# A decoder layer on one core: weight loads, running sums and sample loads around the scan's first group

## The chip, the cores and the metric

The kernel runs on one core of one Trainium2 chip. The metric is the time of one execution on the device in microseconds (us). A core has TensorE (matrix products, PE in the profile; PEld are its weight loads), VectorE (DVE), ScalarE (ACT), GpSimd (POOL) and SyncE (SP), which here only issues DMAs. Each engine works through its own instructions in order and waits on semaphores for the others.

## The reference

One inference step of one layer of a hybrid decoder for two groups of tokens at once: a prompt of 512 tokens and 8 samples of one token each, d_model 1024, all in float32. What matters here is branch B, a state space scan over 32 heads in 8 groups:

```python
proj = h @ w_in                                   # u | z | xBC | dt | gates
xbc  = silu(causal_conv(xbc))                     # 4 taps, x | B | C
dt   = softplus(dt_raw + dt_bias); dA = dt * A    # A = -exp(A_log)
# prompt: chunks of 128 tokens, per group
Acs   = cumsum(dA)                                # "running sums"
decay = exp(Acs[l] - Acs[s]) for s <= l
y_diag = ((C B^T) * decay) @ (x * dt)
states = B^T (exp(Acs[end] - Acs) * x * dt)
h      = h * exp(Acs[end]) + states               # from chunk to chunk
y_off  = C h_prev * exp(Acs)
# samples: one recurrent step from a given state (8 x 32 x 64 x 128)
y = (y_diag + y_off + D * x); y = rmsnorm(y * silu(z)) @ w_ssd_proj
```

A pooling mixer (branch A), the gated sum of the branches, an output projection and a SwiGLU feed-forward network follow, with adaLN modulation throughout. Outputs are both groups' results and the new pooling, convolution and scan states.

## The kernel before, in words

Activations lie transposed: channels on the 128 partitions, the 512 + 8 tokens in a row of 520. Every large product is made of columns: 128 output channels times the 1024 input channels (8 blocks) times 520 tokens in two halves. Float32 is kept by splitting both sides in two rounded parts and adding three products. So each weight block of 128 x 1024, a *unit* of 512 KB, goes the same way: a DMA into a buffer `raw` (L107; there are three, `NRAW`), a cast to the upper part on ScalarE (`whi`, L116), a subtraction on VectorE for the lower part (`wlo`, L117), which frees the buffer, and 48 matrix products on TensorE (L129).

All work stands in a list `plan` of steps with the units that each needs. `perform` goes through it and calls `ahead(n, m)` before each step: the first `n` units are loaded and split, and of the next `m` only the loads are issued. `n` is two units beyond those that the step needs; `m` is `W["loads"]`, which `sp_order(True)` sets to 2 in the middle of group 0.

The order on TensorE is written out everywhere. From `start` to the end of the scan, ScalarE, VectorE and GpSimd are kept to the written order too (`ordered`). SyncE is kept to it from `sp_order(True)` to `sp_order(False)` (`fetched`); before that a planner orders its DMAs by its own estimates.

`start` normalises and modulates the input and works through the first three columns (dt and the two x columns of group 0) block by block. It calls `ahead(3)` before the last three blocks, so the units 0 to 2 (B and C of group 0, the first x column of group 1) are split there. The memory of `start` is then reused: `cvs`, the samples' convolution states (L599), is loaded there, and GpSimd makes `cpre` of it (L608).

After that a loop over the eight groups g of the scan lists these steps: the columns x0, x1 (`xg`), B (`bt`), C (`ct`), each followed by a convolution (`conv`: ScalarE empties the result into `xb` and `v`, L642 and L643, VectorE adds three taps, L647, and the tail, `end`, runs with the next column), and two gate columns zz of the group before. Between the columns stand the steps of three generators:

- `scan(g)` (`step`): transposes (L723, L733), `xdt` (L728) and `xde` (L730), C B^T masked (L740, L742), chunk states (L762 to L769), scores times decays (L748, for group 0 all four together in `scores_first`), products into y (L787, L789, L793).
- `decays(g)` (`decay`): per chunk the exponentials of the running sums on ScalarE (L682 to L694). They need `dec`, the group's running sums broadcast to all partitions, which `dec_load(g)` (L674) loads from DRAM, 1 MB. Odd groups use the tile `aa`, even ones the tile `dec`.
- `sample(g)` (`part`), six steps: write the samples' B and C rows to DRAM (`dbc`, L815 to L818); load half of the states and the C rows (`h`, L803, and `cc`, L804); multiply on GpSimd (L808); reduce on VectorE (L812) and load the other half; multiply; reduce.

The running sums themselves come from `dt_parts`: a chain on VectorE, a write to DRAM (`dacs`, L575), and four DMAs of very small pieces, `dtx` (L585). `tokens_dt` turns them for the scan (`tok`, L618 and L620). `begin(0)` then loads the running sums of groups 0 and 1 one behind the other. Buffers that limit the order: three `raw`, two PSUM tiles `m` for the columns, four PSUM banks `b` for everything else.

Of the kernel before, what the change touches and what calls it, by code (L numbers as in the profile page):

```python
# [52 lines left out]
def tile_decoder(ctx: ExitStack, tc: tile.TileContext, I: dict, O: dict):  # L53
    nc = tc.nc
    ctx.enter_context(tc.manual_schedule(engines={mybir.EngineType.PE}))
    LOOK = 2
# [30 lines left out]
    def urgent():  # L87
        return tc.high_priority(offset=URGENT)
# [75 lines left out]
    def todo(fn, *units):  # L164
        plan.append((units, fn))

    W = {"made": [], "raws": {}}

    def ahead(n, m=0):

        queue, made, raws = W["queue"], W["made"], W["raws"]
        for i in range(len(made), min(n, len(queue))):
            u = queue[i]
            src, pool = (*u, None)[:2] if isinstance(u, tuple) else (u, None)
            with urgent() if count[0] > NU else nullcontext():
                raw = raws.pop(i) if i in raws else load(src)
                made.append(parts(raw, pool))
        for i in range(len(made), min(n + m, len(queue))):
            u = queue[i]
            if i not in raws:  # L180
                raws[i] = load(u[0] if isinstance(u, tuple) else u)

    def perform():
        queue = W["queue"] = [u for us, _ in plan for u in us]
        made = W["made"]
        at = 0
        for us, fn in plan:
            ahead(at + len(us) + (LOOK if at else 0), W.get("loads", 0))
            got = [made[at + i] for i in range(len(us))]
            for i in range(len(us)):  # L190
                made[at + i] = None
            at += len(us)
            fn(*got)
        plan.clear()
# [237 lines left out]
    raws = [ada_rows(0)]  # L432
    wraw = [load(w) for w in (win(72), X0(0), X1(0))]

    def start():
        sp = st
        RB = sp.tile([P, T], F32, name="RB")
        acc = sp.tile([P, T], F32, name="acc1")
        for s in range(1, len(SLICES)):
            raws.append(ada_rows(s))  # L440
        for k in range(KD):
            add_square(sp, acc, xT[:, k], 0, T, k == 0)
        nc.vector.tensor_scalar(cwh, pv[:, PV["cw"][0] : PV["cb"][1]], 0.5, None, ALU.mult)
        ends = {}

        def ada(s, ks=range(KD)):
            m0, m1 = SLICES[s]
            n, q = P, m1 - m0
            if ks[0] == 0:
                ends[s] = bank()  # L450
            for k in ks:
                ada_mm(ends[s], raws[s][:, k], k, n, k == 0, k == KD - 1, 2 * q)
            if ks[-1] == KD - 1:
                with urgent():
                    ends[s] = ada_end(ends[s], n, lambda i: (U_SC1, U_SH1)[i // q] + m0 + i % q, sp, 2 * q)

        def normed(k):
            xn = sp.tile([P, T], F32, tag="xn", name=f"xn{k}", bufs=3)
            (nc.vector if k % 2 == 0 else nc.gpsimd).tensor_tensor(xn, xT[:, k], RB, ALU.mult)
            return xn  # L460

        def modded(s):
            m0, m1 = SLICES[s]
            with urgent():
                ends[s]()
                a1 = mod[:, U_SC1 + m0 : U_SC1 + m1]
                nw = V["n1w"][:, m0:m1].unsqueeze(2).broadcast_to([P, m1 - m0, 9])
                nc.vector.scalar_tensor_tensor(a1, a1, 1.0, nw, ALU.add, ALU.mult)

        def rows(*ks):  # L470
            hs = []
            for k in ks:
                h = sp.tile([P, T], F32, tag="h", name=f"h{k}", bufs=2)
                modulate(h, xn.pop(k), mod[:, U_SC1 + k], mod[:, U_SH1 + k])
                nc.scalar.copy(hh[:, k], h)
                hs.append(h)
            for k in ks:
                if k + 2 < KD:
                    xn[k + 2] = normed(k + 2)
            for k, h in zip(ks, hs):  # L480
                nc.vector.tensor_tensor(hl[:, k], h, hh[:, k].bitcast(F32), ALU.subtract)  # L481

        def products(k, tiles=range(3)):
            for o, w in [(outs[i], ws[i]) for i in tiles]:
                product(o, w, k, hh[:, k], hl[:, k], k == 0, k == KD - 1)


        def warm(n):
            b = bank()
            for _ in range(n):  # L490
                nc.tensor.matmul(b[:, 0:256], cold[:, 0:P], cold, start=True, stop=True)

        warm(WARM[0])
        r = rstd_start(acc, 1024, range(5))
        w0 = parts(wraw[0], "st")
        ada(0)
        modded(0)
        rstd_end(r, range(5), RB)
        warm(WARM[1])
        xn = {k: normed(k) for k in range(2)}  # L500
        rows(0)
        ws = [w0] + [parts(w, "st") for w in wraw[1:]]
        outs = [both(main()), both(main()), pair()]
        products(0, [0])
        ada(1, range(4))
        products(0, [1, 2])
        ada(1, range(4, KD))

        def rest(s):
            modded(s)  # L510
            rows(*range(*SLICES[s]))

        rest(1)
        ada(2)
        products(1)
        rest(2)
        products(2)
        ada(3)
        products(3)
        modded(3)  # L520
        ada(4)
        rows(5, 6)
        products(4)
        rest(4)
        ahead(3)
        for k in range(5, KD):
            products(k)
        first["ps"] = outs
        closed(st_)
# [136 lines left out]
    def dec_load(g):  # L666

        if g >= NG:
            return
        if g % 2:  # L670
            dec = G["aa"][:, 4:8].rearrange("p a b -> p (a b)")[:, 0:2048].rearrange("p (c h l) -> p c h l", c=4, h=4)
        else:
            dec = S["sp"].tile([P, 4, 4, P], F32, tag="dec", name=f"dec{g}")
        nc.sync.dma_start(out=dec, in_=S["dacs"][:, 4 * g : 4 * g + 4, :].unsqueeze(0).broadcast_to([P, 4, 4, P]))  # L674
        S["dec", g] = dec
# [175 lines left out]
    def sp_order(on):  # L851
        def fn():
            if on:
                fetched.__enter__()
                W["loads"] = 2
            else:
                W["loads"] = 0
                fetched.__exit__(None, None, None)

        return fn  # L860
# [10 lines left out]
    def part(g):  # L871
        def fn():
            if g not in samples:
                samples[g] = sample(g)
            next(samples[g], None)

        return fn

    def decay(g, n=1):
        def fn():  # L880
            if g not in exps:
                exps[g] = decays(g)
            for _ in range(n):
                next(exps[g], None)

        return fn
# [35 lines left out]
    def begin(g):  # L922
        def fn():
            if g == 0:
                dec_load(0)
            dec_load(g + 1)
            gens[g] = scan(g, cur["xg"], cur["bt"], cur["ct"])
            if g:
                next(gens[g])

        return fn
# [16 lines left out]
    for g in range(NG):  # L948
        todo(x0(g), *([X0(g)] if g else []))
        if g > 1:  # L950
            todo(step(g - 1))
        if g == 2:
            todo(part(0))
        if g > 1:
            todo(part(g - 1))
        todo(x1(g), *([X1(g)] if g else []))
        if g == 0:
            todo(dt_more)
        elif g == 1:
            todo(step(0))  # L960
            todo(step(0))
            todo(part(0))
        else:
            todo(step(g - 1))
        todo(bb(g), BB(g))
        if g == 0:
            todo(sp_order(True))
            todo(dt_more)
        else:
            if g == 1:  # L970
                todo(step(0))
                todo(decay(0, 3))
            else:
                todo(decay(g))
            todo(part(g - 1))
        todo(cc(g), CC(g))
        if g == 1:
            todo(decay(0))
            todo(scores_first)
        if g:  # L980
            todo(part(g - 1))
            todo(decay(g))
            todo(zz(2 * g - 2), ZZ(2 * g - 2))
            todo(step(g - 1))
            if g == 1:
                todo(decay(1))
            todo(zend(2 * g - 2))
            todo(part(g - 1))
            todo(decay(g))
            todo(zz(2 * g - 1), ZZ(2 * g - 1))  # L990
            todo(step(g - 1))
            todo(zend(2 * g - 1))
            todo(part(g - 1))
            todo(decay(g))
        todo(begin(g))
        if g:
            todo(part(g))
        else:
            todo(flush)
# [576 lines left out]
```

## Time and profile before

| | |
|---|---|
| median of 3 runs | 1124.08 us (1122.76 to 1125.9) |
| the profiled execution | 1125.83 us, of it 1124.1 us from the first to the last instruction (the span) |
| TensorE busy | 1081.5 us, 96% |
| VectorE, ScalarE, GpSimd busy | 700.8, 463.4, 349.0 us |
| mean granted TensorE clock | 0.979 |
| chain that ended last | PE 88%, DVE 3%, DMA 2%, ACT 2% |
| moved by DMA | 165.34 MB, mean 147 GB/s |

The busy time of an engine says how much work it has; the chain that ended last is followed back from the last instruction, at each step to what released it, and says what the end waited for. Times in the views below count from the span's start, and L numbers are lines of the kernel as printed above. A name such as `raw<-in_win` is output and input of an instruction or DMA.

### The profile page before, as it was taken

What the parts mean: (1) busy time and instruction counts of PE and PEld (TensorE: products, weight loads), DVE (VectorE), ACT (ScalarE), POOL (GpSimd) and SP (SyncE); (2) the same over time, 40 slices, a digit from 0 to 9 for tenths busy, and PEclk for the clock granted to TensorE, in tenths of its full rate; (3) what the DMA queues carried; (4) which work ended last, traced back from release to release, by engine and by line L of the source; (5) the groups of instructions that cost most, each with busy time, mean ns of one, the idle gap of its engine ahead of it and who ended that gap; (6) DMA issues with size and microseconds to landing.
All of it is one profiled execution on the core that took longest, in us unless ns stands there. A gap on an engine that the chain in (4) does not pass through costs nothing.

```text
span 1124.1 us, 22173 instructions
## 1 busy us (share of the span) xinstructions
PE 1081.5 (96%) x9345; PEld 1052.6 (94%) x9345; DVE 700.8 (62%) x963; ACT 463.4 (41%) x774; POOL 349.0 (31%) x498
## 2 busy tenths in 40 slices
PE   7988699999999999999999999999999999999995
PEld 6888599999999999999999999899999999999995
DVE  5674778878888798789677745656455553323332
ACT  3245646646646543665333323542222222222220
POOL 1131342432442442100000000389999960000001
PEclk8999699999999999999999999999999999999997
DMA  9327335347346333454435436266666652233212
GB/s 357 145 82 198 92 125 188 110 126 189 109 127 188 120 114 108 151 172 150 150 132 166 154 117 238 97 197 217 206 208 211 190 177 83 88 88 100 85 52 76
DMA packets 58468, 165.34 MB, mean 147 GB/s; under 512 B 10881, under 2 KB 16513, under 8 KB 57601
## 3 DMA queue, kind: packets, MB, share of 16 engines
q1 hardware_dynamic: 51712, 142.96, 39.1%
q0 software_dynamic: 6656, 20.98, 6.1%
q8 instruction: 73, 1.20, 0.4%
q14 instruction: 27, 0.21, 0.1%
HBM read 151.05 MB, written 12.86 MB: 146 GB/s over the span
## 4 chain that ended last, share of the span: by engine, by line
PE 88%; DVE 3%; DMA 2%; issue 2%; ACT 2%; POOL 1%; SPq 0%; POOLq 0%; DVEq 0%; ACTq 0%
PE m L129 77%; PE b L129 4%; PE b L787 2%; DMA raw<-in_win 1%; PE b L762 1%; PE b L789 1%; PE b L301 1%; PE b L207 1%; DVE v L647 1%; PE b L740 1%; PE b L723 1%; DMA xT<-in_xT 0%; ACT whi L116 0%; DMA raw<-in_wada 0%; POOL xn L1238 0%
## 5 line engine op out<-in xcount | busy, mean ns | idle before, releaser
L129 PE MATMUL m<-hh,whi 128*128 128x260 f32 (+1 forms) x1840 | 382.4, 288 | 4.7 <-ACT v L643 3.5
L129 PE MATMUL m<-hl,whi 128*128 128x260 f32 (+1 forms) x1840 | 375.9, 285 | 3.3 <-DVE hl L481 3.1
L129 PE MATMUL m<-hh,wlo 128*128 128x260 f32 (+1 forms) x1840 | 375.6, 285 | 0.0
L117 DVE TENSOR_TENSOR wlo<-raw,whi 128x1024 fp32r<-128x1024 f32 (+2 forms) x169 | 233.7, 1386 | 183.7 <-ACT whi L116 180.8
L116 ACT CAST whi<-raw 128x1024 fp32r<-128x1024 f32 (+2 forms) x169 | 173.0, 1027 | 365.2 <-PE m L129 241.9
L129 PEld LDWEIGHTS m<-hh,whi 128*128 128x128 f32 x1840 | 287.4, 190 | 11.8 <-ACT v L643 3.7
L129 PEld LDWEIGHTS m<-hl,whi 128*128 128x128 f32 x1840 | 286.9, 190 | 4.1 <-DVE hl L481 3.8
L129 PEld LDWEIGHTS m<-hh,wlo 128*128 128x128 f32 x1840 | 287.5, 190 | 0.0
L341 POOL TENSOR_TENSOR r<-me,mhalf 128x5 f32<-128x5 f32 (+2 forms) x6 | 6.4, 1065 | 437.7 <-DVE me L340 437.7
L647 DVE SCALAR_TENSOR_TENSOR v<-xb,cwh,v 128x512 f32<-128x512 f32 x96 | 73.6, 767 | 23.1 <-ACT v L643 21.2
L129 PE MATMUL m<-ah,whi 128*128 128x260 f32 x264 | 53.3, 283 | 0.0
L129 PE MATMUL m<-ah,wlo 128*128 128x260 f32 x264 | 53.1, 283 | 0.0
L129 PE MATMUL m<-al,whi 128*128 128x260 f32 x264 | 53.0, 282 | 0.0
L129 PE MATMUL m<-gh,whi 128*128 128x260 f32 x256 | 52.9, 288 | 0.0
L1342 DVE TENSOR_TENSOR fs<-m,fs 128x520 f32<-128x520 f32 (+2 forms) x23 | 15.5, 676 | 59.1 <-PE m L129 58.3
L129 PE MATMUL m<-gl,whi 128*128 128x260 f32 x256 | 51.4, 282 | 0.0
L129 PE MATMUL m<-gh,wlo 128*128 128x260 f32 x256 | 51.3, 282 | 0.0
L1329 POOL TENSOR_TENSOR ht<-bb,xds 128x512 f32<-128x512 f32 x32 | 46.7, 1460 | 2.2 <-DMA bb<-dbc 1.7
L642 ACT COPY xb<-m 128x520 f32<-128x520 f32 (+1 forms) x31 | 17.8, 575 | 68.7 <-PE m L129 68.7
L808 POOL TENSOR_TENSOR h<-h,cc 128x1024 f32<-128x1024 f32 x16 | 38.3, 2394 | 23.2 <-DMA cc<-dbc 22.2
L1331 POOL TENSOR_TENSOR hs<-hs,ht 128x512 f32<-128x512 f32 x32 | 43.9, 1372 | 0.8
L129 PEld LDWEIGHTS m<-gh,whi 128*128 128x128 f32 x256 | 39.3, 189 | 2.1 <-PE b L301 0.9
(300 smaller groups left out, 1752.4 us busy)
## 6 DMA issues: line engine op xcount, KB each, us to landing
raw<-in_win SPq DMA_DIRECT2D x73, 512.0 KB, 4.8
raw<-in_wfi SPq DMA_DIRECT2D x44, 512.0 KB, 4.3
araw<-in_wada SPq DMA_DIRECT2D x24, 512.0 KB, 4.0
h<-in_sssm SPq DMA_DIRECT2D x16, 512.0 KB, 4.5
raw<-in_wssd SPq DMA_DIRECT2D x16, 512.0 KB, 3.4
hs<-in_sssm POOLq DMA_DIRECT2D x32, 256.0 KB, 4.1
out_ssms<-hs POOLq DMA_DIRECT2D x32, 256.0 KB, 3.6
raw<-in_wfo SPq DMA_DIRECT2D x16, 512.0 KB, 3.5
```

Source lines behind the costliest of these rows:

```text
L116: nc.scalar.copy(hi, raw)
L117: nc.vector.tensor_tensor(lo, raw, hi.bitcast(F32), ALU.subtract)
L129: nc.tensor.matmul(o, a[:, k, c0 : c0 + P], b[:, t0:t1], start=f, stop=e)
L207: nc.tensor.matmul(ps[32 * i : 32 * i + 32, 0:n], sc[:, k], raw[:, n * i : n * i + n], start=first, stop=last)
L301: nc.tensor.matmul(ps[32 * i : 32 * i + 32, 0:256], scr[:, k], w[:, 256 * i : 256 * i + 256], start=k == 0 and j == 0, stop=k == KD - 1 an ...
L642: nc.scalar.copy(shape(xb[:, 3 + t0 : 3 + t1]), o)
L647: nc.vector.scalar_tensor_tensor(v[:, 0:TP], xb[:, k : k + TP], w(k), v[:, 0:TP], ALU.mult, ALU.add)
L787: nc.tensor.matmul(o, xdt[:, c, 2 * i + h], dec[:, c, 2 * i + h], start=c == 0, stop=False)
L808: nc.gpsimd.tensor_tensor(h0, h0, cc.unsqueeze(2).broadcast_to([P, 4, 2, P]), ALU.mult)
L1329: nc.gpsimd.tensor_tensor(t, bb.unsqueeze(2).broadcast_to([P, 2, 2, P]), at(xds), ALU.mult)
L1331: nc.gpsimd.tensor_tensor(h, h, t, ALU.add)
L1342: nc.vector.tensor_tensor(view(s[:, t0:t1]), u, view(s[:, t0:t1]), ALU.mult)
```

## The change

`W["loads"]` is 2 from the beginning, but counts only once units have been made, so that `start` is not changed by it. `start` asks for three more units: the loads of the units 3 to 5 (second x column, B and C of group 1) are issued behind the splitting of the units 0 to 2, in the part where the planner orders SyncE. `begin(g)` loads the next group's running sums only from g = 1 on; those of group 1 are loaded by a step of their own, behind the first three decays of group 0, between the B and C columns of group 1. And in group 1 the second to fifth steps of `sample(0)` stand one place later each: the step behind the B column falls away and one is added behind `begin(1)`.

```diff
-    W = {"made": [], "raws": {}}
+    W = {"made": [], "raws": {}, "loads": 2}
...
-            ahead(at + len(us) + (LOOK if at else 0), W.get("loads", 0))
+            ahead(at + len(us) + (LOOK if at else 0), W["loads"] if made else 0)
...
         rest(4)
-        ahead(3)
+        ahead(3, 3)
         for k in range(5, KD):
...
             if on:
                 fetched.__enter__()
-                W["loads"] = 2
...
             if g == 0:
                 dec_load(0)
-            dec_load(g + 1)
+            if g:
+                dec_load(g + 1)
             gens[g] = scan(g, cur["xg"], cur["bt"], cur["ct"])
...
             if g == 1:
                 todo(step(0))
                 todo(decay(0, 3))
+                todo(lambda: dec_load(1))
             else:
                 todo(decay(g))
-            todo(part(g - 1))
+                todo(part(g - 1))
         todo(cc(g), CC(g))
...
         todo(begin(g))
+        if g == 1:
+            todo(part(0))
         if g:
             todo(part(g))
```

## The prediction

> **What bounds the kernel now.** I read the page's slices first, then who TensorE waited for in the first 300 us, then the chain that ended last in order of time, then each engine's timeline around the wait that matters.
>
> ```profile
> PE   7988699999999999999999999999999999999995
> ```
> ```profile
> PE b L787 <- ACT dec L693: 8.4, 1, 8.4
> PE b L815 <- ACT tok L620: 4.6, 1, 4.6
> ...
> PE b L787 <- DVE dec L748: 2.2, 1, 2.2
> ```
>
> The first row is TensorE's busy share in 40 slices of 28.1 us, the others are waits (engine and line, releaser, us in total, times, longest). From the sixth slice (140 us) to the end TensorE is at nine tenths or more, so a microsecond won before that is kept and one won later on another engine is worth nothing. The idle time lies in slices 0 to 4. Its largest pieces are the two waits of L787, the first group's scan: 8.4 us for ScalarE's decay factors and 2.2 us for VectorE's product of scores and decays. L815 (4.6 us) waits for the copy `tok`. The chain of waits says what set the scan's restart at 123.34:
>
> ```profile
> 85.36 16.38 DMA raw<-in_win
> 101.76 1.06 ACT whi L116
> ...
> 121.57 1.73 DVE dec L748
> 123.34 1.91 PE b L787 x12
> ```
>
> So the restart is set by a weight load that takes 16.38 us to land. ScalarE's timeline (start, length, instruction, idle time before it and its releaser) shows what stands around it:
>
> ```profile
> 88.98 1.04 ACT L116 CAST whi<-raw 128x1024 fp32r<-128x1024 f32 x1 [4.15 <-DMA raw<-in_win]
> ...
> 111.51 1.03 ACT L116 CAST whi<-raw 128x1024 fp32r<-128x1024 f32 x1
> ```
>
> I number the weight units as their queue has them: 0 BB0, 1 CC0, 2 and 3 X0 and X1 of group 1, 4 BB1, 5 CC1, 6 ZZ0, 7 ZZ1, 8 X0 of group 2. The cast at 88.98 is unit 5, with `tok` right behind it. The cast of the chain, at 101.76, is unit 6; behind it on ScalarE stand the three first decays of group 0 and then, at 111.51, the cast of unit 7 and the first state copy, without a pause. What comes early for unit 6 is early for all of them.
>
> Why unit 6 is late is read from SyncE's queue and from the landing times of the same DMAs (last column, us from issue to landing):
>
> ```profile
> 81.69 1.33 SPq L585 DMA_DIRECT2D dtx<-dscr  x1
> 83.06 1.08 SPq L107 DMA_DIRECT2D raw<-in_win  x1
> 84.25 0.49 SPq L674 DMA_DIRECT2D dec<-dacs  x1
> 84.79 0.53 SPq L674 DMA_DIRECT2D aa<-dacs  x1
> ```
> ```profile
> dtx<-dscr SPq DMA_DIRECT2D x1, 32.0 KB, 5.3
> raw<-in_win SPq DMA_DIRECT2D x1, 512.0 KB, 5.9
> dec<-dacs SPq DMA_DIRECT2D x1, 1024.0 KB, 9.8
> aa<-dacs SPq DMA_DIRECT2D x1, 1024.0 KB, 15.7
> ```
>
> Landings: the last `dtx` 86.99, unit 5 88.98, `dec` of group 0 94.05, `dec` of group 1 (in `aa`) 100.5, unit 6, from the chain, 101.76. They come in the order of issue, one after another: 0.5 MB of unit 5 in 1.99 us, the two 1 MB broadcasts in 5.07 and 6.45 us, unit 6 1.26 us after the second.
>
> **The change part by part.**
>
> *Units 3 to 5 asked for in `start` (ahead(3, 3)).* Before, units 3 and 4 were already loaded at 57.99, ahead of the waits of SyncE's written order; only unit 5 sat in that order behind the four `dtx` DMAs:
>
> ```profile
> 53.82 3.50 DVE L117 TENSOR_TENSOR wlo<-raw,whi 128x1024 fp32r<-128x1024 f32 x3 [0.25 <-ACT whi L116]
> 57.56 0.33 SPq L599 DMA_DIRECT2D cvs<-in_sconv  x1
> 57.99 0.85 SPq L107 DMA_DIRECT2D raw<-in_win  x2
> 61.24 0.76 POOL L608 TENSOR_TENSOR cpre<-cvs,cwh 128x256 f32<-128x256 f32 x1 [3.50 <-DMA cvs<-in_sconv]
> 67.95 0.70 DVE L659 SCALAR_TENSOR_TENSOR xg<-t,v 128x520 f32<-128x520 f32 x1
> ```
>
> The three buffers come free as the subtractions of units 0 to 2 end (three in the 3.50 us from 53.82), so the three loads can go out at about 55.0, 56.2 and 57.3. Unit 5 is then in place long before ScalarE reaches its cast, which moves from 88.98 to 84.84 (its 4.15 us of idle go); `tok` moves with it and L815's 4.6 us wait goes. Alone this brings nothing: TensorE only reaches L787 sooner and waits there longer. It matters because unit 5's 0.5 MB, 1.99 us, leave the queue in front of unit 6.
>
> What it costs: these loads may stand ahead of `cvs` in the queue, whose landing releases GpSimd at 61.24 and, through the first conv's tail, VectorE's L659 at 67.95, where VectorE has been busy until that very moment; so a late `cvs` is late everywhere, `dtx` included. Ends: 0 if SyncE's planned order keeps `cvs` first, as it had it; three times 1.26 = 3.8 us if all three are in front and none has drained. Each load has 1.2 us of head start on the next and drains in about 1.26, so at 57.56 only the last is still in the way: 0 to 1.3, I take +0.6.
>
> *Group 1's running sums (dec_load(1)) after decay(0, 3).* One DMA of 1 MB moves on SyncE past the loads of units 6 and 7, the small write `dbc` and the load of unit 8; none of these waits for it. Its 6.45 us leave the queue in front of unit 6. Unit 6 then lands at 86.99 + (5.07 to 6.45, `dec` of group 0) + 1.26 = 93.3 to 94.7; I take 94.0, the middle, since 5.07 may hold some overlap with unit 5. That is 7.8 us before 101.76 (7.1 to 8.5). What could be late next: TensorE's BB1 product, whose output the same step of ScalarE empties. It ends where L740 starts, and moves up by the 4.15 us:
>
> ```profile
> 97.81 1.05 PE L740 MATMUL b<-ct,bt 128*128 128x128 f32 x8
> ```
>
> 97.81 − 4.15 = 93.7, less what TensorE runs slowly after the 4.6 us of idle; so product and weights arrive together and ScalarE's chain shifts by the whole 7.8. Group 1's sums go out at about 89 behind unit 8 and land by about 105; their first reader on ScalarE stands behind group 0's fourth decay, which ends where the chain has L748 (121.57), after the change about 113: 8 us cover it. That cover gone would cost ScalarE one microsecond for one.
>
> *Sample loads of group 0 one step later.* The step's two DMAs (the state `h0`, the `cc` row) leave the place behind unit 8, where SyncE stood still for `dbc` to land; they go behind the group's state write instead. The GpSimd multiply that used them moves from before the second score product to after zend(0):
>
> ```profile
> 120.38 2.35 POOL L808 TENSOR_TENSOR h<-h,cc 128x1024 f32<-128x1024 f32 x1
> L748 DVE TENSOR_TENSOR dec<-dec,cbm x4: 681/684/1716, 119.7 to 123.8; 128x512 f32<-128x512 f32 x4
> ```
>
> Of the four score products three took about 0.68 us; the one at 121.57 took 1.72 us while GpSimd multiplied until 122.73. It is on the chain, and TensorE's 2.2 us wait is for it. Without the multiply beside it, −1.0 us (bounds: 0 if something else slows it, −1.04). The Trainium skill, "SBUF — State Buffer", section "Who interferes with whom", says that a VectorE instruction with two inputs in SBUF and a GpSimd instruction that reads SBUF exclude each other for the whole instruction; the row agrees within a tenth or so (blocked until 122.73, plus 0.68, is 123.4; it ended at 123.29). The same rule speaks against the change as well: it moves the exclusion and does not end it, and by it the second multiply would hold a VectorE instruction for up to its 2.4 us in front of group 2.
>
> What that second half costs, from rows alone:
>
> ```profile
> 129.95 1.21 DVE L812 TENSOR_REDUCE y_s<-h 128x8 f32<-128x1024 f32 x1
> cc<-dbc SPq DMA_DIRECT2D x1, 256.0 KB, 4.4
> 143.96 2.33 DVE L647 SCALAR_TENSOR_TENSOR v<-xb,cwh,v 128x512 f32<-128x512 f32 x3 [1.60 <-ACT v L643]
> 146.97 2.04 POOL L730 TENSOR_TENSOR xde<-xdt,tok 128x512 f32<-128x512 f32 x2 [8.06 <-DVE xdt L728]
> 156.26 1.73 PE b L762 x8
> ```
>
> The first reduction (1.21 us) moves behind zend(1), about 130 to 131 after the shift. Only then do the second half's loads go out; `cc` takes 4.4 us, so GpSimd's second multiply runs at about 136 to 138.4. Behind it on GpSimd stands the memset of x0 of group 2, which VectorE's conv at 143.96 − 8.2 = 135.8 needs: VectorE starts 2.7 us late. GpSimd's `xde` product (146.97, ends 149.0) is due at TensorE's 156.26, 7.3 us of cover, and the other columns have theirs; I take 0 for TensorE (bounds 0 to +2.7, the whole lag). Behind the held SyncE queue stand group 2's running sums and unit 12, each about 4 us later; their readers stand behind two more products of group 2 in ScalarE's order.
>
> *The rest.* Asking for two loads from `start` on changes no other step: until unit 4 is made nothing is left to ask for.
>
> Sum: −7.8 + 0.6 − 1.0 = −8.2 us. The profiled execution took 1125.83 us (its span of 1124.1 and 1.7 around it), which gives 1117.6; the median of the runs, 1124.08, lies 1.75 below it, so the prediction for a median is 1115.9, say 1116.
>
> **The rivals.**
>
> *Short slow stretch, more gain.* After the restart TensorE's granted clock stayed low for 7.8 us:
>
> ```profile
> 127.00:131.10 4.10, 4.10 (x21) 4.10 (x20) 4.07 (x6) 4.00 (x10) 0.32 (x2) 0.50 0.01 2
> 131.10:134.80 3.70, 3.70 (x31) 3.57 (x30) 1.29 (x2) 0.41 (x1) 0.00 (x0) 0.99 0.57 174
> ```
>
> After the 4.6 us idle it took from 90.55 to 93.71, 3.2 us, until a pair of products took 0.41 us again:
>
> ```profile
> 90.55 0.37 PE L815 MATMUL b<-cst,bc_s 128*16 128x128 f32 x1 [4.61 <-ACT tok L620]
> ...
> 93.71 0.41 PE L129 MATMUL m<-hl,whi 128*128 128x260 f32 x2
> ```
> If the new restart at about 115 is like that one, (7.8 − 3.2) × half = 2.3 us more are won: 1113.6. For it: the idle before L787 shrinks to about 6 us. Against: it is still longer than the 4.6. The Trainium skill, "TensorE: Matmul & The Clock Gate", section "Part 1: The HAM clock gate", has half the clock after an idle window of about 3.4 us and full clock after one such window of work, free-running; by it a slow stretch of 3.4 us and about 1114 would come out. The 3.2 us agree with it, the 7.8 us do not.
>
> *`cvs` well behind.* All three loads ahead of it and another half megabyte too: +3.8 to 5 us, 1120. Against: their buffers come free one by one.
>
> *It does not do what it says.* Two of the first six units were already early; if the queue shares its rate among all that is in it, unit 6 lands when it did, and unit 5's gain only lengthens the wait at L787: 1124. Against: five landings in strict order of issue.
>
> *The other side: GpSimd held in front of group 2.* If the second half's loads meet a full queue, as the first half's did, they take
>
> ```profile
> h<-in_sssm SPq DMA_DIRECT2D x1, 512.0 KB, 11.7
> ```
>
> 11.7 us and more instead of 4.4: GpSimd's lag becomes 10 to 13 us, TensorE loses what goes over the 7.3 us of cover, up to 6, and 1122 is left. It ends slower than before only from a lag of some 19 us (7.3 + 8.2 + 3.4), 1127.5. Against: at 131 us the queue holds two weight units at most.
>
> **How the numbers follow.** The forecast 0.60, own range 1114.5 to 1121 (gains of 8.5 + 1.0 and of 7.1 − 1.3 − 2.7); short slow stretch 0.13; `cvs` well behind 0.10; nothing gained 0.07; GpSimd held 0.10, half of it to 1122, half slower. The range 1112 to 1122 leaves out about 0.17. Taking 0.3% (3.4 us) as what a measurement can tell from no change: faster 0.60 + 0.13 + 0.10 = 0.83, same 0.07 + 0.05 = 0.12, slower 0.05.
>
> **What the changed profile would show.** Right: no wait of L815 for `tok`; ScalarE's cast of unit 6 at about 94.5 (94.0 and the 0.6); the second score product at 0.68 us; TensorE's scan restart at about 115; the broadcast into `aa` issued after unit 8. Wrong: the cast of unit 6 still at 100 or later, GpSimd's first `cpre` well after 62.5, or a wait of TensorE between 130 and 170 that was not there.

## Result and profile after

The changed kernel took 1117.85 us (median of 4 runs, 1117.18 to 1118.05), the kernel before 1124.17 us in the runs beside it (4 runs, 1122.76 to 1125.9). The ratio is 0.9942, 95% interval 0.9925 to 0.9959: 6.5 us faster, with an interval of 4.6 to 8.4 (the two medians lie 6.3 apart). The profiled execution took 1118.05 us, its span 1116.3.

The page's slices of TensorE, 27.9 us each, and who TensorE waited for in the first 300 us (engine and line, releaser, us in total, times, longest):

```profile
PE   8988899999999999999999999999999999999995
```
```profile
PE b L787 <- ACT dec L693: 6.3, 1, 6.3
PE m L129 <- ACT v L643: 5.5, 1, 5.5
...
PE b L787 <- DVE dec L748: 1.1, 1, 1.1
```

The wait of L815 for `tok` is gone, L787 waits 6.3 us instead of 8.4 for the decays and 1.1 instead of 2.2 for the score product. One wait grew: the second x column of group 1 (L129, for the first conv's `v`) waits 5.5 us instead of 3.5. The chain of waits, and SyncE's queue with three landing times (last column, us from issue to landing):

```profile
54.99 6.15 DMA cvs<-in_sconv
...
83.40 11.20 DMA raw<-in_win
94.62 1.06 ACT whi L116
...
114.44 0.70 DVE dec L748
115.18 1.90 PE b L787 x12
```
```profile
30.07 24.75 SPq L107 DMA_DIRECT2D raw<-in_win  x6
54.99 0.33 SPq L599 DMA_DIRECT2D cvs<-in_sconv  x1
...
78.13 4.17 SPq L585 DMA_DIRECT2D dtx<-dscr  x4
82.41 0.90 SPq L674 DMA_DIRECT2D dec<-dacs  x1
83.40 4.13 SPq L107 DMA_DIRECT2D raw<-in_win  x2
...
89.33 0.71 SPq L107 DMA_DIRECT2D raw<-in_win  x1
90.08 0.57 SPq L674 DMA_DIRECT2D aa<-dacs  x1
```
```profile
cvs<-in_sconv SPq DMA_DIRECT2D x1, 512.0 KB, 6.2
...
dec<-dacs SPq DMA_DIRECT2D x1, 1024.0 KB, 10.6
```

The scan restarts at 115.18 instead of 123.34, and still on the weight load of unit 6 and its cast at 94.62 (before 101.76). The broadcast into `aa`, group 1's sums, now goes out at 90.08 behind unit 8. `cvs` is issued behind all six unit loads, takes 6.2 us to land and is now a piece of the chain itself.

**A mark inside the trace that says more than the whole time.** The 8.2 us between the two restarts are not all the change's. The end of `start`, where ScalarE takes the dt column's result (L548, same code in both), lies 2.85 us earlier in this execution; the difference arises before anything that the change touched, and begins in the first matrix products. The rows are ScalarE's and TensorE's timelines and the stretch from the beginning to that row (granted clock in the third column from the right), first of before, then of after:

```profile
57.58 1.62 ACT L548 ACTIVATE dtmp<-m,pv 32x128 f32<-32x128 f32 x5 [1.89 <-issue]
```
```profile
14.64 3.19 PE L207 MATMUL b<-araw,sc 128*32 128x128 f32 x32
```
```profile
0.00:57.57 57.57, 48.53 (x471) 42.41 (x472) 33.38 (x79) 19.12 (x31) 7.59 (x9) 0.91 0.64 245
```
```profile
54.73 1.62 ACT L548 ACTIVATE dtmp<-m,pv 32x128 f32<-32x128 f32 x5 [1.90 <-issue]
```
```profile
14.59 1.94 PE L207 MATMUL b<-araw,sc 128*32 128x128 f32 x32
```
```profile
0.00:54.73 54.73, 46.55 (x471) 40.50 (x472) 33.28 (x79) 19.09 (x31) 7.60 (x9) 0.97 0.68 266
```

The same 32 products took 3.19 us in one execution and 1.94 in the other; nearly all of the rest arises where pairs of column products took 0.64 us instead of 0.40, from 36 to 39 us in the kernel before. Over all thirteen traces the end of `start` scatters from 54.4 to 58.2, and it follows the clock granted up to that row: 0.97 in five traces (54.4 to 55.1), 0.94 in four (55.7 to 56.0), 0.91 in four (57.3 to 58.2). The change itself, traced twice, fell once in the first class and once in the second. Whether the edits have any part in it, one trace of each kernel cannot tell: three of the four slowest are the kernels whose running sums were not moved. (The Trainium skill, "TensorE: Matmul & The Clock Gate", section "Part 1: The HAM clock gate", has the clock decided in windows that run freely, so that where the first products fall in one varies from run to run; the two rows fit that, and no run here isolates it.) So everything below counts from that row: restart minus end of `start` was 65.76 us before and is 60.45 after, **5.3 us** less. The rest of the span after the restart is 998.5 to 1001.1 us in all thirteen, without a trend.

### The profile page after: what moved, and what is told of

Its sections match the earlier page's. It is cut to its first block, busy times and chain, and to the rows that moved or that the text cites. A ratio compares the mean times of both kernels' runs of the same rounds, so it can differ in the third digit from the quotient of the medians.

```text
span 1116.3 us, 22172 instructions
## 1 busy us (share of the span) xinstructions
PE 1077.9 (97%) x9345; PEld 1049.3 (94%) x9345; DVE 699.5 (63%) x963; ACT 463.3 (42%) x774; POOL 348.3 (31%) x498
## 4 chain that ended last, share of the span: by engine, by line
PE 84%; DVE 5%; DMA 5%; ACT 2%; issue 2%; POOL 1%; SPq 0%; DVEq 0%; ACTq 0%; POOLq 0%
PE m L129 73%; PE b L129 4%; DMA araw<-in_wada 2%; PE b L787 2%; PE b L762 1%; PE b L789 1%; DMA raw<-in_win 1%; DVE ar L286 1%; PE b L207 1%; ACT aw L285 1%; PE b L301 1%; PE b L740 1%; DMA cvs<-in_sconv 1%; PE b L723 1%; DVE acc L391 0%
## 5 line engine op out<-in xcount | busy, mean ns | idle before, releaser
L129 PE MATMUL m<-hh,whi 128*128 128x260 f32 (+1 forms) x1840 | 381.5, 287 | 7.6 <-ACT v L643 5.5
L129 PE MATMUL m<-hl,whi 128*128 128x260 f32 (+1 forms) x1840 | 375.0, 284 | 3.3 <-DVE hl L481 3.1
L129 PE MATMUL m<-hh,wlo 128*128 128x260 f32 (+1 forms) x1840 | 374.6, 284 | 0.0
L129 PEld LDWEIGHTS m<-hh,whi 128*128 128x128 f32 x1840 | 286.4, 189 | 14.6 <-ACT v L643 5.8
L129 PEld LDWEIGHTS m<-hl,whi 128*128 128x128 f32 x1840 | 286.0, 189 | 4.2 <-DVE hl L481 3.8
L129 PEld LDWEIGHTS m<-hh,wlo 128*128 128x128 f32 x1840 | 286.4, 189 | 0.0
L129 PE MATMUL m<-ah,whi 128*128 128x260 f32 x264 | 53.2, 283 | 0.0
L129 PE MATMUL m<-ah,wlo 128*128 128x260 f32 x264 | 53.1, 282 | 0.0
L129 PE MATMUL m<-al,whi 128*128 128x260 f32 x264 | 53.0, 282 | 0.0
L129 PE MATMUL m<-gh,whi 128*128 128x260 f32 x256 | 52.8, 288 | 0.0
L129 PE MATMUL m<-gl,whi 128*128 128x260 f32 x256 | 51.3, 282 | 0.0
L129 PE MATMUL m<-gh,wlo 128*128 128x260 f32 x256 | 51.3, 282 | 0.0
L129 PEld LDWEIGHTS m<-gh,whi 128*128 128x128 f32 x256 | 39.2, 188 | 2.2 <-PE b L301 0.9
```

Source lines behind the costliest of these rows:

```text
L129: nc.tensor.matmul(o, a[:, k, c0 : c0 + P], b[:, t0:t1], start=f, stop=e)
```

## The experiments

Three theories stood against each other at first: that the running sums moved behind unit 6 make the gain (with the score product); that the loads asked for ahead do, by taking half a megabyte out of the queue; and that the late `cvs` takes part of it back. Each time is a median, its ratio taken to the kernel before on the same chip. The marks are from one trace each, so differences of a microsecond between two rows may be scatter; they are in us from the end of `start`: VectorE's first L659 (all behind `cvs` and the first conv), the issue and duration to landing of group 0's sums (`dec`), how far behind them unit 6 landed, its cast, and the restart.

| run | time, ratio and interval | L659 | `dec` issued, took | unit 6 behind | cast | restart |
|---|---|---|---|---|---|---|
| before | | 10.37 | 26.67, 9.8 | 7.7 | 44.18 | 65.76 |
| the change | 0.9942 (0.9925 to 0.9959) | 12.46 | 27.68, 10.6 | 1.6 | 39.89 | 60.45 |
| the change again | 1118.88, 0.9960 (0.9944 to 0.9975) | 12.78 | 27.98, 10.9 | 1.3 | 40.18 | 60.72 |
| loads only | 1125.86, 1.0012 (1.0000 to 1.0024) | 12.77 | 27.98, 10.2 | 8.7 | 46.83 | 68.40 |
| sums only | 1119.56, 0.9954 (0.9938 to 0.9969) | 10.37 | 26.65, 10.8 | 1.3 | 38.78 | 61.01 |
| samples only | 1123.32, 0.9995 (0.9979 to 1.0011) | 10.49 | 26.71, 10.1 | 8.4 | 45.26 | 65.82 |
| sums and samples | 1118.98, 0.9944 (0.9927 to 0.9961) | 10.52 | 26.82, 10.6 | 2.7 | 40.21 | 60.77 |
| `cvs` first | 1115.64, 0.9935 (0.9914 to 0.9956) | 10.39 | 25.60, 10.5 | 2.5 | 38.58 | 59.12 |
| `cvs` first, spare load | 1117.08, 0.9928 (0.9911 to 0.9945) | 10.61 | 26.98, 10.8 | 3.1 | 40.87 | 61.42 |
| `cvs` first, `dtx` late | 1113.68, 0.9900 (0.9882 to 0.9917) | 10.51 | 25.33, 10.0 | 1.3 | 36.68 | 57.23 |
| `cvs` first, unit 6 first | 1115.08, 0.9909 (0.9891 to 0.9927) | 10.38 | 26.65, 11.0 | ahead | 31.74 | 56.22 |
| unit 6 first, no loads | 1117.91, 0.9945 (0.9934 to 0.9957) | 10.52 | 27.42, 11.6 | ahead | 35.15 | 60.30 |
| all three | 1114.36, 0.9918 (0.9906 to 0.9931) | 10.40 | 25.21, 9.1 | ahead | 32.02 | 56.51 |

**The loads alone.** Only the units asked for ahead, the running sums and sample steps as before.

```diff
-    W = {"made": [], "raws": {}}
+    W = {"made": [], "raws": {}, "loads": 2}
...
-            ahead(at + len(us) + (LOOK if at else 0), W.get("loads", 0))
+            ahead(at + len(us) + (LOOK if at else 0), W["loads"] if made else 0)
...
-        ahead(3)
+        ahead(3, 3)
```

> The weight loads of units 3 to 5 asked for in start, nothing else of the change. Theory Q (unit 6's place in SyncE's queue sets the scan's restart): unit 5's 2 us leave the queue in front of unit 6, but the late convolution state (in the changed kernel it landed 6.2 us after issue instead of 3.6) gives about 2.1 back; ScalarE's 4.15 us wait for unit 5 and L815's 4.6 us wait are gone, and the wait of L787 grows from 8.4 to 11 us or more. Time 1124, between 1122.5 and 1125.5. Rival T (the gain came from unit 5 and the copy tok behind it): L787's wait does not grow, about 4 us are won, 1120.

The time did not fall: 1.0012 (1.0000 to 1.0024), 1125.86 where 1125.5 was the upper end of what was expected. The restart lies 2.6 us later than before's. L659 is 2.4 us late, and the cast of unit 6 lies 34.06 us behind L659 (46.83 − 12.77), before 33.81. So half a megabyte less in the queue did not bring unit 6 earlier at all here, and the late `cvs` came through in full. L787 itself waits 8.9 us for the decays, not the 11 expected; another 2.8 us of waiting fall on a column in front of it, which waits for ScalarE, itself held by the cast of unit 6:

```profile
107.33 0.51 PE L129 MATMUL m<-hh,whi 128*128 128x260 f32 x2 [2.80 <-ACT v L643]
...
123.77 0.69 PE L787 MATMUL b<-dec,xdt 128*64 128x128 f32 x4 [8.87 <-ACT dec L693]
```

**The running sums alone.**

```diff
-            dec_load(g + 1)
+            if g:
+                dec_load(g + 1)
...
                 todo(decay(0, 3))
+                todo(lambda: dec_load(1))
```

> Only the running sums of group 1 later. Theory Q: unit 6 lands about 6.5 us earlier, near 95.3 on the clock of the profile before; but unit 5 and tok stay late, so TensorE's BB1 product still ends at 97.8 and ScalarE can empty it only then: the chain moves by about 4.9 us, time 1119.3 (1118 to 1121). Rival S (the DMA queue shares its rate and the order in it does not matter): unit 6 lands when it did, 1124. Rival T: no gain, since unit 5 is where it was, 1124.

Restart 4.75 us earlier, ratio 0.9954: nearly all of the change's gain in one moved DMA. Here unit 6 is so early that ScalarE waits for TensorE's BB1 product in between (its timeline):

```profile
94.50 1.05 ACT L116 CAST whi<-raw 128x1024 fp32r<-128x1024 f32 x1 [3.73 <-DMA raw<-in_win]
96.10 0.59 ACT L642 COPY xb<-m 128x520 f32<-128x520 f32 x1 [0.55 <-PE m L129]
```

The wait for the load is over at 94.50, and the copy of the product, which could start at 95.5, starts at 96.10: BB1 is late because TensorE waited 4.5 us for `tok`, as before.

**The sample loads alone.**

```diff
-            todo(part(g - 1))
+                todo(part(g - 1))            # now under else: not in group 1
...
         todo(begin(g))
+        if g == 1:
+            todo(part(0))
```

> Only the sample steps of group 0 one place later. Theory: the second score product falls from 1.72 to about 0.69 us because GpSimd no longer multiplies beside it, and the restart comes 1.0 us earlier: 1123.2. GpSimd's second multiply stands in front of group 2's memset and VectorE waits some 3 to 5 us there, without a wait of TensorE. Rival G: TensorE pays for that wait, up to 2.7 us: 1124 to 1126.

```profile
PE b L787 <- DVE dec L748: 1.1, 1, 1.1
```

TensorE's wait for the second score product is 1.1 instead of 2.2 us, as in the whole change. From cast to restart it took 20.56 us, before 21.58: 1.02 less. The restart itself did not move (65.82), since unit 6 fell 1.1 us later in this execution, and the ratio, 0.9995 (0.9979 to 1.0011), cannot tell one microsecond from none. VectorE waited 4.5 us in front of group 2 and TensorE did not, as expected.

**Everything but the loads.** The two edits above together.

> The change without its first part: the loads of units 3 to 5 as in the kernel before, sums and samples moved. From the end of start (ScalarE's first L548) to the restart of L787 it was 65.8 us before, 60.4 with the whole change, 61.0 with the sums alone. Theory L (asking for the loads in start costs more, by the late convolution state, than it brings): 61.0 less the 1.0 us of the score product, 60.0, a little under the whole change; time 1118 to 1118.5. Rival (the loads are a necessary part of the gain): over 62, 1120 or more.

0.9944, and 60.77 at the restart: no difference from the whole change (0.9942; 60.45 and 60.72). The 60.0 expected was missed because unit 6 landed 2.7 us behind `dec` here, where it was 1.3 with the sums alone. So the loads asked for ahead bring nothing in sum, though `tok` is copied 2.2 us earlier with them (30.17 us after the end of `start` in the change, 32.43 here).

**The loads, but `cvs` ahead of them.** The change, with the loads of units 3 to 5 asked for after `cvs`.

```diff
         rest(4)
-        ahead(3, 3)
+        ahead(3)
...
-        nc.sync.dma_start(out=cvs, in_=I["sconv"])
+        with urgent():
+            nc.sync.dma_start(out=cvs, in_=I["sconv"])
+        ahead(3, 3)
```

> The whole change, with the load of the convolution states issued ahead of the loads of units 3 to 5. Theory Q with the late state as its cost: the state lands 3.6 us after its issue instead of 6.2, VectorE's L659 follows the end of start by 10.4 us instead of 12.5, and everything up to the restart moves by 2.1 us: 1115.8 (1115 to 1116.8). TensorE's wait for X1 falls from 5.5 to about 3.5 us. Rival V (VectorE's own work or something else holds L659, the state's lateness is hidden): 1117.9.

```profile
cvs<-in_sconv SPq DMA_DIRECT2D x1, 512.0 KB, 3.7
```

`cvs` lands in 3.7 us again, L659 is back at 10.39, and the restart is 1.3 us before the change's (59.12 against 60.45), not the 2.1 expected: `dec` goes out 2.1 us earlier, but unit 6 lands 2.5 us behind it instead of 1.6. Against the run without the loads ahead (60.77) they now win 1.65 us, 1.2 of them in the issue of `dec`; the ratios of the two runs, 0.9935 and 0.9944, cannot be told apart.

**Half a megabyte put back.** The same, with a load of 512 KB that nothing reads, issued where unit 5 stood before, in front of group 0's sums.

```diff
             if g == 0:
+                spare = ...          # 128 x 1024, the place of a tile not yet used
+                nc.sync.dma_start(out=spare, in_=win(0))
                 dec_load(0)
```

> As the run with the convolution states first, plus one load of half a megabyte that nobody reads, issued where unit 5's load stood before: between dtx and group 0's running sums. Its time is that of this extra load. By the prediction's step it delays unit 6 by 2.0 us: restart 61.1, 1117.7. By what the first runs showed (group 0's running sums landed 7.1, 7.1, 6.7, 8.1 and 7.0 us after the last dtx, with unit 5 in between in the first and fourth): 0 to 1.1 us, restart 59.1 to 60.2, 1115.7 to 1116.8.

```profile
dec<-dacs SPq DMA_DIRECT2D x1, 1024.0 KB, 10.8
spare<-in_win SPq DMA_DIRECT2D x1, 512.0 KB, 5.3
```

The broadcast takes 10.8 us from its issue with the spare load in front, 10.5 without (the run before). What the load costs is its issue: the broadcast goes out 1.4 us later (26.98 against 25.60), 0.2 of them already there at L659. The restart is 2.3 us later; of the 0.9 that is left, 0.3 is in the broadcast and 0.6 in how far unit 6 landed behind it, which differs from 1.3 to 3.1 us over these runs without a cause that they show. The whole time does not show the cost at all: 0.9928 (0.9911 to 0.9945) with the load, 0.9935 (0.9914 to 0.9956) without. That it cost 2.3 us rests on one trace of each. That a load in front of `dec` moves its issue by about 1.1 us holds in all traces with `dtx` in its place: counted from L659, `dec` goes out at 16.2 to 16.4 us behind one load and at 15.2 behind none.

**`dtx` out of the way.** The run with `cvs` first, and the four `dtx` DMAs (32 KB each, in very small pieces) issued after `begin(2)`.

```diff
-        for half in range(2):        # in dt_parts: the four dtx DMAs
...
+        if g == 2:
+            todo(dtx_late)           # the same four
```

> The whole change, the convolution states first, and the four DMAs of small pieces (dtx) moved behind group 2. Theory Q with dtx in the way: group 0's running sums are issued hardly earlier (they wait for the transposes of tokens_dt), but land 8.4 us after issue as group 2's did, instead of 10.5, and unit 6 follows: restart 57 us after the end of start, 1113.6. Rival D (the running sums take their 10.5 us by themselves): 59 and 1115.5.

The best ratio of all, 0.9900, with the restart at 57.23, close to the 57 expected, but not for the reason that I had: the broadcast took 10.0 us from its issue, not 8.4. Its issue came only 0.3 us sooner, as expected, although SyncE was free of 4.2 us of `dtx`. What held it is in SyncE's waits:

```profile
SPq L679 <- PE b L623: 4.8, 1, 4.8
```

L623 in that kernel (L618 in the others) is the transposition of `tokens_dt`: the tile for group 0's sums presumably takes memory that it reads from. It stands behind the third of eight blocks of TensorE's second x column, which itself waits for the first conv. Of the 1.9 us won at the restart over `cvs` first, 0.3 is the issue, 0.5 the broadcast, 1.2 unit 6 closer behind it. The last differs by as much between other runs, so that the mark came out at 57 is luck in good part.

**Unit 6 in front of the sums.** The run with `cvs` first, and group 0's sums asked for at the start of x0 of group 1, behind the load of unit 6.

```diff
         def fn(*w):                  # x0(g)
+            if g == 1:
+                dec_load(0)
...
-            if g == 0:
-                dec_load(0)          # begin(0)
```

> The whole change, the convolution states ahead of units 3 to 5, and the load of unit 6 ahead of group 0's running sums: the same bytes in another order. Theory Q (SyncE's queue is served in order, and unit 6 is what ScalarE waits for): unit 6 lands about 6 us earlier, ScalarE empties BB1 as soon as TensorE has it, and the restart comes 2.7 us before that of the run with the states first (59.1 to 56.4 us after the end of start): 1113.0. Then the landing of the running sums or BB1 holds the decays. Rival S (the transfers in flight share the rate, order does not matter): 59.1 and 1115.7.

```profile
raw<-in_win SPq DMA_DIRECT2D x1, 512.0 KB, 5.4
```
```profile
89.06 1.05 ACT L116 CAST whi<-raw 128x1024 fp32r<-128x1024 f32 x1
93.92 0.59 ACT L644 COPY xb<-m 128x520 f32<-128x520 f32 x1 [3.82 <-PE m L129]
```

Unit 6 lands in 5.4 us, its cast runs without a wait, and no DMA sets the restart any more: as with the sums alone, ScalarE waits for TensorE's BB1, here 3.82 us. The next in line is close: `dec` landed at 94.97 (83.97 + 11.0), 0.65 us before ScalarE's first use of it. Restart 56.22, against 56.4 expected; ratio 0.9909. The median, 1115.08, is 2.1 us above the 1113.0 expected, and the interval (0.9891 to 0.9927) meets that of `cvs` first (0.9914 to 0.9956), so that this order is better rests on the marks.

**The same without the loads ahead.** Sums, samples and unit 6 first, the loads as before.

> Sums and samples moved, the loads of units 3 to 5 as before the change, and unit 6 loaded ahead of group 0's running sums. If the loads in start are worth nothing in any company, this gains as much as the same swap did with them and the states first (2.9 us): from 60.8 to 57.9 us after the end of start, 1115.5. If they are worth something as soon as unit 6 is no longer what ScalarE waits for (because unit 5 and tok then set when TensorE's BB1 product ends, as in the run with the sums alone), the restart comes at 59 to 60, 1117 to 1118.

```profile
89.80 1.04 ACT L116 CAST whi<-raw 128x1024 fp32r<-128x1024 f32 x1
95.33 0.59 ACT L642 COPY xb<-m 128x520 f32<-128x520 f32 x1 [4.49 <-PE m L129]
```

The cast of unit 6 is early here too, and it brings almost nothing (60.30 against 60.77, 0.9945 against 0.9944): the copy of BB1 comes 40.68 us after the end of `start` (95.33 − 54.65), in the run before 36.60 (93.92 − 57.32). Of the 4.1 us between them, 2.5 are BB1's later beginning, most of it a wait for `tok`, and 1.5 its longer run, since its first pairs take 0.64 us instead of 0.40:

```profile
87.73 0.27 PE L815 MATMUL b<-cst,bc_s 128*16 128x128 f32 x1 [2.05 <-ACT tok L620]
...
88.16 0.64 PE L129 MATMUL m<-hl,whi 128*128 128x260 f32 x2
```

Here the loads ahead count: they bring BB1 forward, once unit 6 is not later than BB1 anyway. The whole times agree (0.9945, 0.9934 to 0.9957, against 0.9909, 0.9891 to 0.9927).

**The change again, and all three.** The change unaltered beside them, and `cvs` first, `dtx` late and unit 6 first together.

> The changed kernel once more, beside the others of this call: 1117.9. Its second profile shows how far the same program's own numbers scatter: end of start to restart 60.4 us again if they do not, and group 0's running sums 10.0 to 11.0 us after their issue with unit 6 1.3 to 3.0 us behind them, as in the runs so far.

> The whole change with the convolution states first, unit 6 ahead of group 0's running sums, and dtx moved behind group 2. In the run with the first two the chain on ScalarE already followed BB1's end without a wait, so dtx has nothing left to give there: restart 56.2 us after the end of start, as without, 1113 to 1114. If dtx costs elsewhere (its tiny pieces beside group 2's loads), 1115 or more.

The change repeats its marks within 0.4 us (restart 60.72 against 60.45). Its ratio, 0.9960 (0.9944 to 0.9975), is a gain of 4.5 us, less than the 6.5 of the first runs; the two intervals overlap. All three together give 0.9918 and 56.51: `dtx` adds nothing once BB1 sets the restart. The three best versions, 0.9900, 0.9909 and 0.9918, cannot be told apart. Each beats the kernel before by 9 to 11 us and lies ahead of the change (0.9942, 0.9960); the best one's interval does not meet the change's.

## Why the prediction held, and where its steps failed

The forecast, 1116.0, lies 1.85 us below the measured median, and the range holds it. The mechanism was right in the main: unit 6 sets the restart, and group 1's sums in front of it were most of the wait. Two of the three terms of the sum were 2.9 us too favourable together; the range was wide enough to hold that. The interval of the whole time (4.6 to 8.4 us) holds the predicted 8.2 as well as the 5.3 counted below; only the trace tells them apart. Point by point, from the end of `start`:

- *Unit 6 earlier by 7.8.* Measured from L659, 6.4 (33.81 to 27.43). **This term was mis-sized, and its part for unit 5 failed.** It took 1.99 us of bytes out of the queue; what came out was 1.1 us of issuing: `dec` goes out 16.30 us behind L659 with unit 5 in front (before, and sums and samples) and 15.22 without (the change). The broadcast then took 0.8 us more than before (10.6 against 9.8), not less. In all kernels it took 9.1 to 11.6 us from its own issue, with 512 KB of unit 5, of a spare load or of unit 6 in front of it, or nothing at all, so the strict order of landings that the prediction read from five rows was not a queue of bytes for a weight load in front of the broadcast. The sums' own part was right: unit 6 lands 1.6 us behind `dec` instead of 7.7, 6.1 us won of 6.45 counted. −1.1 + 0.8 − 6.1 is the 6.4.
- *A late `cvs`, +0.6 (0 to 1.3).* **The second term that was mis-sized**: +2.1 at L659 (12.46 against 10.37), 2.4 in two other traces. The step took each load to drain in 1.26 us with 1.2 us of head start. Three loads issued 1.13 us apart kept the DMA engines full (0.90 to 0.99 of their time from 54 to 60 us), and `cvs` behind them took 6.2 us instead of 3.6. SyncE's planned order did not keep `cvs` first. VectorE, busy until then before, now waits for it:

```profile
67.19 0.70 DVE L659 SCALAR_TENSOR_TENSOR xg<-t,v 128x520 f32<-128x520 f32 x1 [2.40 <-ACT t L658]
```

- *Second score product −1.0.* Exact: 0.70 us in the chain instead of 1.73. The sum of the measured parts is −6.4 + 2.1 − 1.0 = −5.3, where −8.2 was predicted. That the traced restart, 115.18, agrees with the predicted 115 is chance: 2.85 us of it are the early end of `start`.
- *The loads in sum.* The prediction said of the early unit 5 that "Alone this brings nothing"; right, and with the late `cvs` the restart comes 2.6 us later. Within the change its +2.1 and −1.1 leave a loss of about 1 us that is inside the scatter of unit 6's landing.
- *GpSimd in front of group 2, 0 (0 to +2.7).* Right. The rows of GpSimd and VectorE, and TensorE's busy time (us of window, then busy us of PE first, in two stretches):

```profile
136.15 2.39 POOL L808 TENSOR_TENSOR h<-h,cc 128x1024 f32<-128x1024 f32 x1 [7.98 <-DMA cc<-dbc]
138.48 0.10 POOL L638 MEMSET xb<- 128x3 f32 x1
```
```profile
121.18 2.57 DVE L846 SCALAR_TENSOR_TENSOR y<-gz,y 128x512 f32<-128x512 f32 x1
...
138.61 2.33 DVE L647 SCALAR_TENSOR_TENSOR v<-xb,cwh,v 128x512 f32<-128x512 f32 x3 [4.81 <-POOL xb L638]
```
```profile
132.00:492.00 360.00, 359.50 (x3166) 351.93 (x3165) 291.69 (x408) 199.42 (x367) 121.86 (x211) 1.00 0.47 143
```

The second multiply ran at 136.15 to 138.54, forecast at 136 to 138.4, and VectorE waited 4.81 us for the memset behind it, not 2.7. That the multiply met the predicted position is chance too: from the end of `start` it came 3.0 us later than forecast (81.4 against 78.4), as the restart did. TensorE is busy 359.5 of the next 360 us: the cover of 7.3 us held. The exclusion moved, as the rule of the Trainium skill ("SBUF — State Buffer", section "Who interferes with whom") has it: the first multiply, 120.82 to 123.21, now holds L846, 2.57 us where the same line took 0.69 at 129.05, but off the chain.
- *Short slow stretch.* Fell. Windows around the restart (granted clock in the third column from the right):

```profile
115.18:117.10 1.92, 1.92 (x14) 0.99 (x16) 1.92 (x4) 1.89 (x5) 0.00 (x0) 0.50 0.77 296
...
121.00:123.00 2.00, 2.00 (x13) 2.00 (x12) 1.97 (x2) 1.94 (x6) 2.00 (x1) 0.61 0.46 180
123.00:125.00 2.00, 2.00 (x19) 2.00 (x18) 1.33 (x2) 1.39 (x2) 0.20 (x1) 1.00 0.00 0
```

Half clock from 115.18 into the stretch 121 to 123, some 7.4 us, before 7.8. The idle time before it (6.3 instead of 8.4) shrank by 2.1 us, the stretch by 0.4. The Trainium skill ("TensorE: Matmul & The Clock Gate", section "Part 1: The HAM clock gate") has the full clock come back after one busy window of about 3.4 us; the 7.4 us do not agree with it.
- *`cvs` well behind, and nothing gained.* The first was partly true in mechanism: all three loads were in front, but at 2.1 us, not 3.8 to 5. The second fell with unit 6's landing. *The other side* did not come: the second half's `cc` row landed 4.8 us after its issue at 131.32 (GpSimd's start at 136.15), not 11.7.
- *What would show it.* Seen as written: no wait for `tok`, the cast at 94.62, the score product at 0.70, `aa` behind unit 8, `cpre` at 61.21 (not after 62.5), no new wait of TensorE at 130 to 170. But the mark for `cpre` was an absolute time, and the early end of `start` hid the delay: from there it is 6.48 us, before 3.66. Not foreseen: the wait of the second x column, 3.5 to 5.5 us, which is the late `cvs` as TensorE sees it.

Open: why the 1 MB broadcast takes some 10 us from its issue whatever stands in front of it, and what moves unit 6's landing by up to 1.8 us behind it from one execution to the next.

## What to carry to other kernels

Before a load is moved forward in a queue, look at what it now stands in front of: here half a megabyte asked for early was worth 1.1 us of issue time, and cost 2.1 us on a load behind it that nobody had counted as urgent. Take one change to the chain at a time and name the wait that is next: the loads ahead were worth nothing as the change had them, and 4 us once `cvs` and unit 6 stood in front. And where the beginning of a kernel scatters by nearly 4 us, compare distances from a row in the trace that both kernels share, not the positions themselves.

## What the runs showed of the hardware that I had not expected

- A broadcast of 1 MB to all partitions (group 0's sums) took 9.1 to 11.6 us from its own issue, with 0 or 512 KB issued just before it; its time followed its issue, not the bytes ahead. Another broadcast in front did count: group 1's sums took 15.7 to 16.8 us right behind group 0's (three traces), 9.8 to 12.9 where they went out later (ten).
- After a wait of 3.5 us TensorE came back at full rate (0.40 us for a pair of products) in one execution and not in another (0.64), and after 5.5 us it did not. Rows of the first pair behind the wait and the next, first before, then after, then with `cvs` first (its L645 is L643):

```profile
78.27 0.51 PE L129 MATMUL m<-hh,whi 128*128 128x260 f32 x2 [3.48 <-ACT v L643]
78.61 0.40 PE L129 MATMUL m<-hl,whi 128*128 128x260 f32 x2
```
```profile
77.49 0.80 PE L129 MATMUL m<-hh,whi 128*128 128x260 f32 x2 [5.54 <-ACT v L643]
78.09 0.64 PE L129 MATMUL m<-hl,whi 128*128 128x260 f32 x2
```
```profile
75.12 0.80 PE L129 MATMUL m<-hh,whi 128*128 128x260 f32 x2 [3.48 <-ACT v L645]
75.72 0.64 PE L129 MATMUL m<-hl,whi 128*128 128x260 f32 x2
```

- The same 32 matrix products (L207) took 3.19 us in one execution and 1.94 in another, and the end of `start` came anywhere within 3.8 us, in three classes by the clock granted until then (0.91, 0.94, 0.97).
